# A hybrid encoder layer: the mixer walked head by head, or block by block

## The chip, the cores and the metric

One core of a Trainium2 chip runs the whole layer in one launch. The metric is device microseconds of one execution. Before the change three runs gave a median of 3042.16 us (3032.88 to 3047.0).

## What is computed

The input is 2048 tokens of width 1024. The layer normalises them (`layer_norm`), mixes them along the sequence, attends to 256 memory tokens and applies a squared-ReLU MLP, each with a scaled residual and a LayerNorm:

```python
h   = layer_norm(x, ln_in_g, ln_in_b)
mix = hybrid_mixer(h, ...)                       # 4 mLSTM heads || 4 GLA heads, one in-projection
h   = layer_norm(ALPHA * h + mix, ln1_g, ln1_b)
xa  = memory_cross_attention(h, mem, wq, wk, wv, wo)
h   = layer_norm(ALPHA * h + xa, ln2_g, ln2_b)
ff  = squared_relu_mlp(h, w_ff1, w_ff2)
h   = layer_norm(ALPHA * h + ff, ln3_g, ln3_b)
```

In the mixer, `proj = h @ w_in` gives q, k, v and an output gate for each mLSTM head, q, k, v and a gate for each GLA head, and a few gate columns. Each head then runs a recurrence along the sequence in chunks: a state is carried from chunk to chunk, so within a head the order of time is fixed, while heads are independent of one another.

## The kernel before

**Number format.** A float32 value goes to TensorE (PE) as a pair of float16 tensors, high and low part; `mm3` (lines 149 to 154) multiplies a pair with a pair in three matmuls. Weights are brought into this form by `prep` (line 136): a load of 1 MB into the one staging tile `stg` (`load_stage`, line 117), the largest magnitude on VectorE (line 110) and over partitions on POOL (line 114), a power of two from it, the high part on ScalarE (line 129) and the low part on VectorE (line 130).

**The units.** The tokens stand in four blocks of 512. A unit is one mLSTM head, or a pair of GLA heads, on one block: 6 head groups, 24 units, listed in `units` (line 809) head group by head group, and within a group block by block. The step of unit u is the recurrence `rec(u)` followed by the in-projection of unit u+3 (`LOOK`, line 830). `m_inproj` makes q, k (with a short convolution), v and the gate of an mLSTM head; `g_inproj` does it for a GLA pair. `m_pre` (line 401) loads the broadcast rows mb and scb and forms the scores, `m_rec` (line 427) walks the chunks; `g_rec` (line 565) builds its decayed scores in seven levels. `y_out` stores the result (line 477). A head group's weights are prepared once, one to two units ahead, and stay in SBUF for its four blocks.

**The front.** All 16 token tiles are normalised first (`ln_in`, line 225), the transposed float16 pairs of the four blocks are kept in SBUF (`hT`), and `gates` and `gate_math` (line 332) compute the gate columns of all 2048 tokens. Beside this the kernel folds the cross-attention weights with the memory tokens: eight folds, each two preparations (`x_w`), `x_a` (keys or values of a head) and `x_b` (their product with the query or output weight), stored to DRAM. Four folds stand between the LayerNorm tiles, with two extra staging slabs for the first, and four in the first four steps of the loop:

```python
        for b in (2, 3):
            x_w(nx)
            x_a(nx)
            for i in range(CPB):
                ln_in(b * CPB + i)
            x_b(nx)
            nx += 1
            gates(b)
            inproj(b - 1)
        gate_math()
```

**The passage to the next stage.** After the last GLA unit of the list, eight units before the end, `b_out_weights` (line 745) and `b_x_weights` (line 774) prepare the output weights and load the folded weights; then `s1`, `s2`, `s3` run the output projection, the cross-attention and LayerNorms tile by tile, and the MLP follows.

**What sets the order.** The kernel is written as one program; when it is built, a scheduler orders each engine's instructions and the DMA queue of SP by program order as priority, as soon as operands and a free buffer are there in its own model of time. So an instruction may go ahead of earlier ones, within the number of buffers of its tile. On the chip each engine and queue runs its own order, waiting where something is late. Nearly all loads, stores and transposing DMAs go through SP's queue.

Of the kernel before, what the change touches and what calls it, by code (L numbers as in the profile page):

```python
# [9 lines left out]
F32 = mybir.dt.float32  # L10
# [26 lines left out]
PF0 = 2  # L37
PF = 1
MA = 0
XO = 1  # L40
GA = 2
XE = 1
NX = 5
NHS = 3
# [13 lines left out]
def layer_kernel(ctx: ExitStack, tc, a, out):  # L58
# [6 lines left out]
    wsp = ctx.enter_context(tc.tile_pool(name="wsp", bufs=4))  # L65
    big = ctx.enter_context(tc.tile_pool(name="big", bufs=4))
# [11 lines left out]

    def slab(shape, dt):
        return big.tile(shape, dt, name="slab")  # L80
# [10 lines left out]
    nm_d = dram.tile([64, P], F32, name="nm_d")  # L91
    sc_d = dram.tile([64, P], F32, name="sc_d")
    glr_d = dram.tile([16, T], F32, name="glr_d")
# [38 lines left out]
    def w_pair(pool=None):  # L132
        pool = pool or wsp
        return pool.tile([P, 2048], F16, name="whi"), pool.tile([P, 2048], F16, name="wlo")
# [76 lines left out]
    with ExitStack() as actx:  # L211
        ca = actx.enter_context(tc.tile_pool(name="ca", bufs=1))
        wk = actx.enter_context(tc.tile_pool(name="wk", bufs=2))
        WPOOL = False
        hT = [slab([P, CPB, 2, KC, P], F16) for b in range(2)]

        pxctx, p1ctx = ExitStack(), ExitStack()
        px = pxctx.enter_context(tc.tile_pool(name="px", bufs=1, reuse_waits="tile", side="right"))
        p1 = p1ctx.enter_context(tc.tile_pool(name="p1", bufs=1, reuse_waits="tile", side="right"))
        est = slab([P, 2, 2048], F32)  # L220
        ew = slab([P, 4, 2048], F16)
        gt, bt = gb_load(p1, a["ln_in_g"], a["ln_in_b"], "in")
        inv_h0, ai_h0 = ln_scale(gt, bt, "h0")

        def ln_in(i):
            x = p1.tile([P, D], F32, name="x", bufs=NX)
            nc.sync.dma_start(x, a["x"][i * P:(i + 1) * P, :])
            layer_norm(x, gt, bt)
            b, ii = divmod(i, CPB)
            hs = p1.tile([P, 2, D], F16, name="hs", bufs=NHS)  # L230
# [15 lines left out]
        li = p1.tile([64, P], F32, name="li")  # L246
        lf = p1.tile([64, P], F32, name="lf")
        gbias = p1.tile([64, 2], F32, name="gbias")
# [14 lines left out]
        def gates(b):  # L263
# [3 lines left out]
            gs = p1.tile([48, TB], F32, name="gs")  # L267
            nc.scalar.activation(gs, pg[0:48, :], AF.Copy, scale=inv_g[0:48])
            for h in range(4):
                for r, dst in ((h, li), (4 + h, lf)):  # L270
                    nc.sync.dma_start(dst[h * 16 + b * 4:h * 16 + b * 4 + 4, :],
                                      gs[r:r + 1, :].rearrange("o (c t) -> o c t", c=4))
            nc.sync.dma_start(glr_d[:, b * TB:(b + 1) * TB], gs[32:48, :])
# [21 lines left out]
        def m_weights(h):  # L295
            qk = prep(a["w_mix"][2 * h], inv_h0, WPOOL)
            vo = prep(a["w_mix"][2 * h + 1], inv_h0, WPOOL)
            return qk, vo

        def m_inproj(h, b, w):  # L300
            (qh, ql, qv), (vh, vl, vv) = w
            qk = []
            for j in range(2):
# [4 lines left out]
                else:  # L308
                    nc.gpsimd.tensor_copy(raw[:, 0:3], raw_prev[j])
                raw_prev[j] = wk.tile([P, 3], F32, name=f"halo{j}")  # L310
                nc.gpsimd.tensor_copy(raw_prev[j], raw[:, TB:TB + 3])
# [18 lines left out]
        gcols = {}  # L330

        def gate_math():
            x = p1.tile([64, P], F32, name="gm_x")
            y = p1.tile([64, P], F32, name="gm_y")
            bb = p1.tile([64, P], F32, name="gm_b")
            one = p1.tile([64, P], F32, name="gm_1")
            cc = p1.tile([64, P], F32, name="gm_c")
            nc.vector.memset(one, 1.0)
# [6 lines left out]
            nc.vector.tensor_tensor_scan(bb, one, x, 0.0, ALU.mult, ALU.add)  # L345
# [4 lines left out]
            nc.tensor.transpose(pr[0:1, 0:64], bb[:, P - 1:P], ident[0:64, 0:64])  # L350
            nc.tensor.transpose(pr[0:1, 64:128], cm[:, P - 1:P], ident[0:64, 0:64])
            row = p1.tile([1, 5 * 64], F32, name="gm_row")
            nc.vector.tensor_copy(row[:, 0:128], pr[0:1, 0:128])
            nc.vector.tensor_tensor(row[:, 128:192], row[:, 0:64], row[:, 64:128], ALU.add)
            for h in range(4):
                nc.vector.tensor_tensor_scan(row[:, 192 + h * 16:192 + h * 16 + 16], row[:, h * 16:h * 16 + 16],
                                             row[:, 128 + h * 16:128 + h * 16 + 16], 0.0, ALU.add, ALU.max)
            nc.vector.memset(row[:, 256:320], 0.0)
            nc.vector.tensor_copy(row[:, 256:320].rearrange("p (h c) -> p h c", h=4)[:, :, 1:16],
                                  row[:, 192:256].rearrange("p (h c) -> p h c", h=4)[:, :, 0:15])  # L360
            pc = ps_s()
            nc.tensor.matmul(pc[0:64, 0:1], lhsT=row[:, 256:320], rhs=one[0:1, 0:1], start=True, stop=True)
# [762 lines left out]
```

## Time and profile before

| | |
|---|---|
| median of three runs | 3042.16 us (3032.88 to 3047.0) |
| profiled execution | span 3025.0 us from first to last instruction; its own time is not given beside it |
| PE busy | 2802.6 us |
| VectorE (DVE) busy | 1898.4 us |
| ScalarE (ACT) busy | 886.2 us |
| POOL busy | 416.1 us |
| mean granted TensorE clock | 0.963 |

A row of a window gives, for each engine, the us in which it was busy and the number of its instructions, then the granted clock of PE (1.00 is 2.4 GHz, 0.50 is 1.2 GHz), the mean busy share of the 16 DMA engines, and GB/s. A timeline row gives start and duration in us, engine, line and operation; what stands in brackets is the idle time before it and who ended it. Busy times of PE cover pipelined matmuls and are not a measure of its peak.

### The profile page before, as it was taken

What the parts mean: (1) busy time and instruction counts of PE and PEld (TensorE: products, weight loads), DVE (VectorE), ACT (ScalarE), POOL (GpSimd) and SP (SyncE); (2) the same over time, 40 slices, a digit from 0 to 9 for tenths busy, and PEclk for the clock granted to TensorE, in tenths of its full rate; (3) what the DMA queues carried; (4) which work ended last, traced back from release to release, by engine and by line L of the source; (5) the groups of instructions that cost most, each with busy time, mean ns of one, the idle gap of its engine ahead of it and who ended that gap; (6) DMA issues with size and microseconds to landing.
All of it is one profiled execution on the core that took longest, in us unless ns stands there. A gap on an engine that the chain in (4) does not pass through costs nothing.

```text
span 3025.0 us, 40992 instructions
## 1 busy us (share of the span) xinstructions
PE 2802.6 (93%) x16666; PEld 1576.8 (52%) x16666; DVE 1898.4 (63%) x3875; ACT 886.2 (29%) x1281; POOL 416.1 (14%) x565
## 2 busy tenths in 40 slices
PE   3579989989988898999999999999999999999997
PEld 2346667665666674565565444444444444444442
DVE  8946774656777666665665555555555555555468
ACT  3335444434445443223232211111111111111110
POOL 1102123323433221111111000000000000000011
PEclk8789999989999999999999999999999999999998
DMA  7832230100012334333437600000000000000001
GB/s 241 241 112 86 105 104 29 38 25 23 9 42 68 125 122 105 82 107 91 112 103 190 181 28 28 28 28 28 17 26 15 28 29 28 28 28 28 15 32 80
DMA packets 221693, 214.63 MB, mean 71 GB/s; under 512 B 171760, under 2 KB 188672, under 8 KB 212800
## 3 DMA queue, kind: packets, MB, share of 16 engines
q1 hardware_dynamic: 214592, 186.84, 21.0%
q0 software_dynamic: 6912, 25.17, 2.3%
q8 instruction: 130, 2.13, 0.3%
q14 instruction: 59, 0.48, 0.0%
HBM read 119.44 MB, written 50.53 MB: 56 GB/s over the span
## 4 chain that ended last, share of the span: by engine, by line
PE 69%; DVE 15%; issue 6%; POOL 3%; DMA 3%; ACT 2%; SPq 1%; POOLq 0%; ACTq 0%; DVEq 0%
PE mm L152 12%; PE mm L154 12%; PE mm L153 12%; PE s L152 9%; PE s L154 9%; PE s L153 8%; PE o L152 1%; PE o L153 1%; PE o L154 1%; DVE wmx L110 1%; DVE st L181 1%; DVE qk L316 1%; SPq L204 1%; DVE wlo L130 1%; DVE slab L1036 1%
## 5 line engine op out<-in xcount | busy, mean ns | idle before, releaser
L1036 DVE SCALAR_TENSOR_TENSOR slab<-s,uiv,slab 128x512 f32<-128x512 f32 x512 | 371.4, 744 | 45.0 <-PE s L154 44.8
L152 PE MATMUL s<-whi,uh 128*128 128x512 f16 x1024 | 389.6, 380 | 5.8 <-ACT uh L129 5.1
L152 PE MATMUL mm<-h2T,whi 128*128 128x512 f16 x1024 | 389.3, 380 | 2.5 <-DMA h2T<-h_d 2.5
L154 PE MATMUL s<-whi,ul 128*128 128x512 f16 x1024 | 387.8, 380 | 1.7 <-DVE ul L130 1.7
L153 PE MATMUL s<-wlo,uh 128*128 128x512 f16 x1024 | 389.3, 380 | 0.0
L153 PE MATMUL mm<-h2T,whi 128*128 128x512 f16 x1024 | 389.2, 380 | 0.0
L154 PE MATMUL mm<-h2T,wlo 128*128 128x512 f16 x1024 | 389.1, 380 | 0.0
L981 DVE CUSTOM_DVE_ANT_0 z<-z 128x512 f32<-128x512 f32 x128 | 88.2, 689 | 427.0 <-ACT z L980 427.0
L980 ACT ACTIVATE z<-mm,winv 128x512 f32<-128x512 f32 x128 | 87.9, 687 | 883.7 <-PE mm L154 883.7
L154 PEld LDWEIGHTS <-wlo 128*128 128x128 f16 x2064 | 203.8, 99 | 182.0 <-issue 9.6
L153 PEld LDWEIGHTS <-whi 128*128 128x128 f16 x1808 | 179.1, 99 | 219.4 <-issue 33.1
L152 PEld LDWEIGHTS <-whi 128*128 128x128 f16 x1808 | 179.0, 99 | 216.1 <-issue 14.0
L152 PE MATMUL mm<-whi,slab 128*128 128x256 f16 x1024 | 279.9, 274 | 12.5 <-ACT whi L129 7.3
L153 PE MATMUL mm<-wlo,slab 128*128 128x256 f16 x1024 | 279.9, 273 | 2.7 <-DVE wlo L130 2.7
L154 PE MATMUL mm<-whi,slab 128*128 128x256 f16 x1024 | 279.9, 273 | 0.0
L110 DVE TENSOR_REDUCE wmx<-stg 128x1 f32<-128x2048 f32 (+1 forms) x63 | 141.8, 2252 | 59.6 <-DMA stg<-in_w_ff 31.2
L152 PEld LDWEIGHTS <-uh 128*128 128x128 f16 x1024 | 100.3, 98 | 127.7 <-ACT uh L129 7.3
L154 PEld LDWEIGHTS <-ul 128*128 128x128 f16 x1024 | 99.9, 98 | 124.9 <-DVE ul L130 5.2
L130 DVE SCALAR_TENSOR_TENSOR wlo<-stg,w_s,whi 128x2048 f16<-128x2048 f32 x58 | 136.5, 2354 | 45.2 <-ACT whi L129 45.2
L114 POOL PARTITION_ALL_REDUCE amx<-umx x64 | 23.0, 360 | 1024.9 <-DVE umx L987 1013.1
L153 PEld LDWEIGHTS <-uh 128*128 128x128 f16 x1024 | 100.3, 98 | 121.1 <-issue 1.1
L152 PE MATMUL mm<-slab,whi 128*128 128x512 f16 x384 | 151.2, 394 | 0.4 <-ACT sg L325 0.4
(333 smaller groups left out, 5277.7 us busy)
## 6 DMA issues: line engine op xcount, KB each, us to landing
stg<-in_w_ff SPq DMA_DIRECT2D x32, 1024.0 KB
stg<-in_w_x SPq DMA_DIRECT2D x14, 1024.0 KB
stg<-in_w_mix SPq DMA_DIRECT2D x14, 1024.0 KB
x<-in_x SPq DMA_DIRECT2D x16, 512.0 KB
h_d<-x SPq DMA_DIRECT2D x16, 512.0 KB
y_d<-yh SPq DMA_DIRECT2D x32, 256.0 KB
r<-h_d POOLq DMA_DIRECT2D x16, 512.0 KB, 3.8
h_d<-hs POOLq DMA_DIRECT2D x16, 512.0 KB, 3.0
```

The costliest lines, as they stand in the source:

```text
L110: nc.vector.tensor_reduce(dst, src, axis=AX.X, op=ALU.max, apply_absolute_value=True)
L114: nc.gpsimd.partition_all_reduce(r, mx, P, bass_isa.ReduceOp.absmax)
L130: nc.vector.scalar_tensor_tensor(lo, stg, s, hi, ALU.mult, ALU.subtract)
L152: nc.tensor.matmul(psum, lhsT=lh, rhs=rh, start=(i == 0), stop=False)
L153: nc.tensor.matmul(psum, lhsT=lh, rhs=rl, start=False, stop=False)
L154: nc.tensor.matmul(psum, lhsT=ll, rhs=rh, start=False, stop=(i == n - 1))
L181: nc.vector.bn_stats(st[:, i, :], x[:, i * 512:(i + 1) * 512])
L204: nc.sync.dma_start_transpose(dst, src)
L316: nc.vector.scalar_tensor_tensor(cv, raw[:, t:t + TB], cj[:, t:t + 1], cv, ALU.mult, ALU.add)
L980: nc.scalar.activation(z[:, f], pz, AF.Relu, scale=w1[2])
L981: nc.vector.tensor_tensor_reduce(z[:, f], z[:, f], z[:, f], 1.0, 0.0, ALU.mult, ALU.max, mx[:, f:f + 1])
L1036: nc.vector.scalar_tensor_tensor(acc[ii][:, ns], po, iv, acc[ii][:, ns], ALU.mult, ALU.add)
```

## The change

The list of units is turned round: all head groups of a block, then the next block, with mLSTM and GLA units alternating.

```diff
+LOOK = 3
+UNITS = (("m", 0), ("g", 0), ("m", 1), ("m", 2), ("g", 1), ("m", 3))
+LAST = (("g", 0), ("m", 0), ("g", 1), ("m", 1), ("m", 2), ("m", 3))
-        units = [u + (b,) for u in (("m", 0), ("m", 1), ("g", 0), ("g", 1), ("m", 2), ("m", 3)) for b in range(NB)]
+        units = [u + (b,) for b in range(NB) for u in (UNITS if b < NB - 1 else LAST)]
```

The 14 in-projection weights are prepared in block 0 and stored; in the other blocks each unit loads them again, one unit ahead, into five pairs of buffers (before, four):

```diff
+        def mix_w(n, b):
+            if b == 0:
+                hi, lo, v = prep(a["w_mix"][n])
...
+                nc.sync.dma_start(wmix_d[n][0], hi)
+                nc.sync.dma_start(wmix_d[n][1], lo)
+            else:
+                hi, lo = w_pair()
+                nc.sync.dma_start(hi, wmix_d[n][0])
+                nc.sync.dma_start(lo, wmix_d[n][1])
+            return hi, lo, wscale[n]
```

The front normalises four tiles; the other blocks' LayerNorms, gates and gate mathematics (now on 16 rows of one block, with the running maximum carried) stand in the loop. The folds start in the step in which block 3's gates are done, and the output weights are prepared in steps 7 to 11, stored, and loaded again after the loop:

```diff
+        for i in range(2):
             ln_in(i)
+        wcur[0] = unit_w(0)
...
+        gates(0)
+        inproj(0)
+        g_setup(p2)
+        gate_math(0)
+        for u in range(1, LOOK):
+            inproj(u)
...
+        for u in range(-3, len(units)):
+            if u >= 0:
+                if u + GA < len(units) and units[u + GA][0] == "g":
+                    g_gate(u + GA)
+                rec(u)
+            b, k = divmod(u + 3, NU)
+            if b + 1 < NB:
+                if k < 2:
+                    for i in range(2):
+                        ln_in((b + 1) * CPB + 2 * k + i)
+                if k == 2:
+                    gates(b + 1)
+                    gate_math(b + 1)
+                    if b + 1 == NB - 1:
+                        p1ctx.close()
+                        x_mem(pxctx.enter_context(tc.tile_pool(name="px", bufs=1, reuse_waits="tile")))
+                        x_w(0)
+            if u >= 0 and u + LOOK < len(units):
+                inproj(u + LOOK)
+            if 7 <= u < 12:
+                out_w(u - 7)
+            if ("w", nx) in xm:
+                x_a(nx)
+                x_b(nx)
+                nx += 1
+                if nx < 8:
+                    x_w(nx)
+        pxctx.close()
...
+    wo, inv_m, g1, b1, inv_h1, ai_h1 = b_out_weights(bw)
+    wqk, vo = b_x_weights()
+    s1(0, bw)
+    s1(1, bw)
```

Two blocks of `hT` are kept instead of four. The two early staging slabs and the folds' own staging tile go, so all preparations use the one tile `stg`. Several buffers are fewer (`NX` 5 to 3, `NHS` 3 to 1, `lx` 4 to 3, `lxh` and `lxl` 3 to 2, `v2` and `sg2` 3 to 2, the GLA score tiles 2 to 1), and the recurrent states of all heads are held at once. The pools of the later stages change sides in SBUF.

## Rows read from the trace of the kernel before

**Rows 1.** The page's busy times and shares of the span, all engines.

```profile
PE 2802.6 (93%) x16666; PEld 1576.8 (52%) x16666; DVE 1898.4 (63%) x3875; ACT 886.2 (29%) x1281; POOL 416.1 (14%) x565
```

**Rows 2.** Windows of the front and of the stages after the mixer.

```profile
core 0: us, PE busy (x) PEld busy (x) DVE busy (x) ACT busy (x) POOL busy (x), PEclk, DMA share, GB/s
0.00:150.00 150.00, 73.53 (x408) 44.52 (x408) 135.55 (x218) 51.15 (x52) 22.29 (x42) 0.83 0.80 241
1180.00:3025.00 1845.00, 1810.51 (x9059) 886.17 (x9056) 1079.83 (x2065) 376.60 (x551) 118.00 (x183) 0.99 0.20 57
```

**Rows 3.** Line 415, first matmuls of each mLSTM recurrence: count, durations, first and last start.

```profile
L415 PE MATMUL s<-qk,qk x128: 272/276/422, 248.0 to 1129.2; 128*128 128x128 f32 x128
```

**Rows 4.** Windows of the mixer's stretches, columns as in rows 2.

```profile
248.00:541.60 293.60, 265.61 (x1883) 193.16 (x1882) 193.30 (x451) 132.17 (x197) 73.63 (x95) 0.97 0.24 83
541.60:979.60 438.00, 398.27 (x3693) 281.86 (x3691) 301.84 (x727) 197.71 (x302) 149.22 (x167) 0.92 0.10 31
979.60:1108.70 129.10, 116.90 (x779) 83.47 (x777) 86.78 (x193) 64.44 (x95) 31.11 (x46) 0.95 0.36 124
```

**Rows 5.** Timeline of SP: y stores that end the 8th, 16th, 21st and 24th step.

```profile
541.55 0.39 SPq L477 DMA_DIRECT2D y_d<-yh  x1
...
979.58 0.39 SPq L477 DMA_DIRECT2D y_d<-yh  x1
...
1108.68 0.39 SPq L477 DMA_DIRECT2D y_d<-yh  x1
...
1161.90 0.53 SPq L477 DMA_DIRECT2D y_d<-yh  x1
```

**Rows 6.** Timeline of PE inside an in-projection: start, duration, operation.

```profile
1109.03 0.38 PE L153 MATMUL mm<-slab,whi 128*128 128x512 f16 x1
1109.24 0.38 PE L154 MATMUL mm<-slab,wlo 128*128 128x512 f16 x1
1109.46 0.27 PE L152 MATMUL mm<-whi,slab 128*128 128x256 f16 x1
1109.57 0.27 PE L153 MATMUL mm<-wlo,slab 128*128 128x256 f16 x1
```

**Rows 7.** Groups by line, 0 to 1300 us, DVE: LayerNorm of the input and weight preparation.

```profile
L110 DVE TENSOR_REDUCE wmx<-stg 128x1 f32<-128x2048 f32 x31 | 70.5, 2278 | 28.4 <-DMA stg<-in_w_mix 23.4 <-DMA stg<-in_w_x 4.9
...
L130 DVE SCALAR_TENSOR_TENSOR wlo<-stg,w_s,whi 128x2048 f16<-128x2048 f32 x26 | 61.3, 2363 | 21.6 <-ACT whi L129 21.6
...
L181 DVE BATCH_NORM_STATS2 st<-x 128x6 f32<-128x512 f32 x32 | 21.1, 673 | 0.3 <-DMA x<-in_x 0.3
...
L193 DVE SCALAR_TENSOR_TENSOR x<-x,rs,b_in 128x1024 f32<-128x1024 f32 x16 | 21.0, 1344 | 5.1 <-POOL rs L184 5.1
...
L192 DVE SCALAR_TENSOR_TENSOR x<-x,mv,g_in 128x1024 f32<-128x1024 f32 x16 | 20.4, 1276 | 0.0
...
L201 DVE TENSOR_TENSOR hs<-x,hs 128x1024 f16<-128x1024 f32 x16 | 19.4, 1217 | 0.3 <-ACT hs L200 0.3
```

**Rows 8.** Timeline of SP: two loads into the staging tile, back to back.

```profile
599.13 0.33 SPq L120 DMA_DIRECT2D stg<-in_w_mix  x1
...
614.33 0.35 SPq L120 DMA_DIRECT2D stg<-in_w_mix  x1
```

**Rows 9.** Timelines of SP and POOL, window of 3 us: a 2 MB burst ahead of scb.

```profile
1070.15 1.93 SPq L782 DMA_DIRECT2D slab<-wqk_d  x4
...
1074.89 0.32 SPq L408 DMA_DIRECT2D scb<-sc_d  x1
...
1079.30 1.38 POOL L412 TENSOR_TENSOR scb<-scb,qk 128x512 f32<-128x512 f32 x1 [0.64 <-DMA scb<-sc_d]
...
1073.00:1076.00 3.00, 3.00 (x22) 2.14 (x21) 1.70 (x8) 2.57 (x5) 0.87 (x1) 1.00 1.03 410
```

**Rows 10.** Waits of SP's queue, 160 to 1140 us: total, times, longest.

```profile
SPq L120 <- DVE wlo L130: 197.7, 18, 38.8
```

More of the change, by code (lines that the diff above doesn't have):

```diff
@@ L77, in ps_o @@
         return ps.tile([P, 512], F32, name="o", bufs=2)
+    big = [None]
+    wsp = [None]
     def slab(shape, dt):
-        return big.tile(shape, dt, name="slab")
+        return big[0].tile(shape, dt, name="slab")
     ident = const.tile([P, P], F32, name="ident")
@@ L330, in layer_kernel, with gate_math @@
         gcols = {}
[L332 to L338, printed above, removed]
+        mlast = [None]
+        def gate_math(b):
+            li, lf = gif.pop(b)
+            x = p1.tile([16, P], F32, name="gm_x")
+            y = p1.tile([16, P], F32, name="gm_y")
+            bb = p1.tile([16, P], F32, name="gm_b")
+            cc = p1.tile([16, P], F32, name="gm_c")
+            one = ones
             nc.vector.tensor_scalar(li, li, gbias[:, 0:1], None, ALU.add)
@@ L495, in g_setup @@
             nc.vector.tensor_copy(idm, ident)
-            G["one"] = p2.tile([P, P], F32, name="one")
-            nc.vector.memset(G["one"], 1.0)
-            G["AT"] = [[p2.tile([P, CPB, P], F32, name=f"AT{i}{j}") for j in range(2)] for i in range(2)]
+            G["one"] = ones
+            G["AT"] = [[p2.tile([P, CPB, P], F32, name=f"AT{j}") for j in range(2)]]
             for r_ in G["AT"]:
@@ L718, in x_b @@
             h, side = divmod(n, 2)
-            w1, w2, wo_ = xm.pop(("w", n))
+            w1, w2 = xm.pop(("w", n))
             kh, kl = xm.pop(("k", n))
             oh, ol = (t.rearrange("p (k n) -> p k n", k=2) for t in w2[:2])
-            if wo_:
-                hi, lo = (wo_.tile([P, 2048], F16, name=f"xo{j}", bufs=1) for j in range(2))
-            else:
-                hi, lo = w_pair()
+            hi, lo = x_pair()
             for u in range(4):
@@ L743, in x_b, with out_w @@
             nc.sync.dma_start(dst[1], lo)
+        wo_d = [dram.tile([2, P, 2048], F16, name=f"wo_d{i}") for i in range(4)]
+        wsc_o = {}
+        def out_w(step):
+            if step < 2:
+                stg = load_stage(a["w_out"][step])
+                wsc_o["mx", step] = mx = sm.tile([P, 1], F32, name=f"womx{step}")
+                absmax(mx, stg)
+                if step == 0:
+                    return
+                mx1 = sm.tile([P, 1], F32, name="wmx")
+                nc.vector.tensor_tensor(mx1, wsc_o["mx", 0], mx, ALU.max)
+                wsc_o["m"] = pow2(all_max(mx1), "wo", bufs=1, pool=const)
+                i, s = 1, wsc_o["m"][0]
+            elif step == 2:
+                stg = load_stage(a["w_out"][0])
+                i, s = 0, wsc_o["m"][0]
+            else:
+                i = step - 1
+                stg = load_stage(a["w_out"][i])
+                mx1 = sm.tile([P, 1], F32, name="wmx")
+                absmax(mx1, stg)
+                s, v = wsc_o[i] = pow2(all_max(mx1), f"wo{i}", bufs=1, pool=const)
+            hi, lo = w_pair()
+            split_with(stg, s, hi, lo)
+            nc.sync.dma_start(wo_d[i][0], hi)
+            nc.sync.dma_start(wo_d[i][1], lo)
@@ L745, in b_out_weights @@
         def b_out_weights(bw):
             wo = [None] * 8
[L747 to L756 removed]
+            for i in range(4):
@@ L828, in rec @@
                 g_rec(h, b, blks.pop(u), u)
-        LOOK = 3
-        x_mem()
-        x_w(0, True, False)
+        ones = ca.tile([P, P], F32, name="ones")
+        nc.vector.memset(ones, 1.0)
         for i in range(2):
             ln_in(i)
-        x_a(0)
+        wcur[0] = unit_w(0)
         for i in range(2, CPB):
             ln_in(i)
-        x_b(0)
-        x_w(1, True)
         gates(0)
-        for i in range(CPB, CPB + 2):
-            ln_in(i)
-        x_a(1)
-        for i in range(CPB + 2, 2 * CPB):
-            ln_in(i)
@@ new lines, in layer_kernel @@
+        g_setup(p2)
+        gate_math(0)
+        for u in range(1, LOOK):
+            inproj(u)
+        for u in range(min(GA, len(units))):
+            if units[u][0] == "g":
+                g_gate(u)
+        nx = 0
+        NU = len(UNITS)
+        for u in range(-3, len(units)):
[20 more added lines that the diff above has]
+            if ("w", nx) in xm:
```

312 lines of the change are left out of this document (128 added, 184 removed).

## Prediction

> **What bounds the kernel now.** I read the page's busy shares first, then the windows by stage, then the stretches of the mixer, and last the rows that price its steps. TensorE (PE) is busy for most of the span [rows 1], so the question is where it is not. From 1180 us on it is busy 1810.5 of 1845 us at clock 0.99 [rows 2]; the change touches nothing there but pool places, so I cost that stage at nothing. The slack lies before. In the first 150 us PE is busy 73.5 us at a granted clock of 0.83, while VectorE (DVE) is busy 135.6 us, 90% [rows 2]: this stretch is DVE's, for all 16 input LayerNorms stand in it and the first recurrence starts only at 248.0 us [rows 3]. After that PE is busy some 90%: 265.6 of 293.6 us, 398.3 of 438 us at clock 0.92 (the GLA recurrences), 116.9 of 129.1 us [rows 4]. So there are two places to gain: work that could run while the LayerNorms run, and the GLA stretch.
>
> **Prices of the steps before.** A step is the recurrence of unit u with the in-projection of unit u+3. The stores of y mark them [rows 5]. Five steps with mLSTM (m) in both parts take 979.58 to 1108.68 us: 25.8 us each. The last three, without in-projection, take 53.2 us. Matmuls of 512 columns follow each other every 0.215 us, those of 256 every 0.11 us [rows 6], so a GLA (g) in-projection (48 and 192 matmuls) is 10.5 us longer than an m one (48 and 96). The eight g recurrences take 438.0 us, 54.75 each; five of them run beside a g in-projection, so a g recurrence costs 54.75 - 25.8 - 5/8 x 10.5 = 22.4 us more than an m one. The first eight steps take 541.55 - 248.0 = 293.5 us; 8 x 25.8 + 3 x 10.5 = 237.9 of them are plain steps, which leaves 55.6 for the four weight folds of that stretch with their weight preparation: 13.9 us a fold. (PE's own part of a fold is 96 matmuls of 256 columns, 10.5 us, so this price is some PE work and a little wait.)
>
> **Part one, the front.** Only four tiles are normalised before the first in-projection, and block 1's four beside units 1 to 3. A LayerNorm tile costs DVE 2 x 0.673 + 1.276 + 1.344 + 1.217 and small ones, 5.6 us; preparing a weight costs it 2.28 + 2.36 and five small operations, 5.3 us [rows 7]. All 14 mixer weights are now prepared in block 0. DVE's work until unit 5's step begins: units 0 to 4 at the DVE time per step of the m and g stretches, 86.8/5 = 17.4 and 301.8/8 = 37.7 us [rows 4], 3 x 17.4 + 2 x 37.7 = 128; 14 x 5.3 = 74; eight tiles, 45; convolutions of units ahead and set-up, some 16: together 263 us. At the 90% that DVE reached before in such a stretch this ends at 291 us. The other bound, the one staging tile, is nearer than it was, since the second staging slab goes: two loads into it stand 15.2 us apart [rows 8], 14 x 15.2 = 213 us, and the mask and gate weights some 15 more. It ends earlier, so DVE sets 291 us.
>
> **Part two, the rest of the mixer.** From unit 5 there are 16 steps with an in-projection, 5 of them of g, 6 g recurrences, and the three last: 16 x 25.8 + 5 x 10.5 + 6 x 22.4 + 53.2 = 653 us. The pairs g with g and m with m become g with m and m with g, which in these prices gives the same sum. All eight folds come here (before, four stood in the LayerNorm front, where PE was idle): 8 x 13.9 = 111 us. The gate projections of blocks 2 and 3: 2 x 24 x 0.215 = 10 us. The gate mathematics, four short chains on 16 partitions for one on 64, and the LayerNorms of blocks 2 and 3 (45 us of DVE) I cost at nothing: they are issued three units or more ahead, beside stretches where DVE is busy 66 to 69% [rows 4]; uncovered they would be 45 us. Sum: 291 + 653 + 111 + 10 = 1065 us for the last y store, against 1161.9 before [rows 5]: 97 us less.
>
> **Part three, what is added.** First, 14 MB of stored weights and 42 MB of reloads (two 0.5 MB halves per weight, 18 units). DMA was busy 10 to 36% in these stretches [rows 4]; 56 MB over 1065 us is 53 GB/s, and a burst of 2 MB ran at 410 GB/s [rows 9]. The bytes are hidden. What could show is the queue: SP issues in its order, and a reload that waits for a free weight pair holds up the mb and scb loads of the next recurrence, on which POOL, then DVE, then PE wait. Before, a load waiting for the staging tile held SP 197.7 us in 18 times, 11 us each [rows 10], while scb was used 4.4 us after its issue, after a wait of 0.6 us behind a 2 MB burst [rows 9]. Bounds: 0 (the pair was freed a unit earlier) and 18 x 8 = 144 us (11 less some 3 us of slack). I take 12, nearer to 0, because five pairs hold any two neighbouring units and the burst row shows 0.6. Second, the folds: the two halves now follow each other at once, and 12 steps (8 m, 4 g, 290 us of DVE) get 8 x 2 x 5.3 = 85 us of it for fold weights, 5 x 4.6 = 23 for the output weights and 22 of LayerNorm: 420 of some 550 us, 76%, and the folds' evictions on top. Bounds 0 and 60 (one idle chain of 7 us per fold); I take 20, as in the steps with folds before DVE was busy 66% and PE still 90% [rows 4]. Third, the passage to the next stage: output weights, fold results and LN1 vectors, some 13 MB, are loaded only when the mixer's pools are free. At 410 GB/s that is 32 us; their places come free with the last in-projection, about the 53 us of the last three steps earlier. Bounds 0 and 32; I take 12.
>
> Gain 97 - 12 - 20 - 12 = 53, rounded down to 52 us. The profile's span is 3025.0 us; the execution's own time is not given beside it, the median of the three runs lies 17.2 us above it (the fastest 7.9), and I keep 17.2 as what lies around the span and between runs: 3025 - 52 + 17 = **2990 us**.
>
> **The rivals.** (a) *The mixing fills the gaps of the GLA stretch.* For it: PE is idle 40 of 438 us and its clock 0.92 there [rows 4], and now every g recurrence has m units around it. Against: only three buffers of q, k and v let units run ahead, and PE's order is fixed at build. If a g recurrence cost only some 12 us over an m one, six of them save 60: 2930 us. The Trainium skill's page Perfetto Trace Analysis, section Optimization Strategy, advises interleaving regimes that have different busiest engines, which is this rival. By that rule the trace agrees for the front (90% DVE), while in the GLA stretch DVE at 69% was no full regime of its own.
> (b) *The cover is lost.* Passage and folds both cost their upper bounds, 32 and 60 us, and block 0 slips by a few: nothing is left, about 3040 us. For it: one staging tile for everything, and a fold's chain crosses five engines. Against: steps with folds before, at 13.9 us a fold.
> (c) *Slower: the reloads block SP.* Place: SP's queue, ahead of the mb and scb loads. Price: 8 us in each of the 18 reloading units, 144 in place of my 12, so 80 us over before: about 3122 us; milder, 3080. It decides from 3.6 us a unit on, where the remaining gain of 64 us is gone. For it: the 11 us holds [rows 10]. Against: the 0.6 us [rows 9]. The Trainium skill's page DMA: Bandwidth & Descriptors, section Queues, rings and completion order, says that each DMA engine consumes a sequencer's descriptors in ring order, which speaks against the change: a 3 MB reload ahead of scb would then cost its full 7.5 us at the measured rate, 135 us in 18 units, so about 3113 us. By that rule the trace agrees only in part: scb behind 2 MB was 0.6 us late.
> (d) That it does not do what it says: the blocks are walked by the new unit list, so only the order of issue could keep the old front; I give it no chance of its own.
>
> **How the numbers follow.** Forecast 0.45, (a) 0.17, (b) 0.18, (c) 0.20. Around the forecast the bounds of part three reach about +/- 40 us. The range runs from (a) at 2930 to the milder half of (c), 3085; left out are half of (a) and half of (c), just under 0.2. About 0.5%, 15 us, is what a measurement can tell from no change here. Faster by more: 0.45 x 0.95 + 0.17 + a little of (b), 0.62. Slower by more: (c) and a little of (b), 0.23. Between: 0.15. The forecast's own range is 2950 to 3030.
>
> **What would show it.** Right: the first recurrence's matmuls near 100 us, the fifth y store before 300, the last near 1110; DVE near 90% until 290; the stage after it as long as before. Part two is wrong if steps between reloads are longer than 26 us (m). Rival (c) shows as POOL or DVE waiting for the mb or scb load, and SP's waits on weight reloads; (b) as PE waiting for kh or for the output weights. A last y store after 1162 makes the prediction wrong.

## Result: slower by 3.4%, and the profile after

The changed kernel takes 3140.56 us (median of four runs, 3134.47 to 3162.05) against 3044.58 us for the kernel before on the same chip: a ratio of 1.0338, 95% interval 1.0292 to 1.0384. The prediction was 2990 us; it was wrong in sign, and the time lies above its range of 2930 to 3085. The profiled span is 3134.0 us, 109 us more than before. Busy time of the engines, from the page, beside [rows 1]:

```profile
PE 2815.1 (90%) x16696; PEld 1585.3 (51%) x16696; DVE 1897.4 (61%) x3956; ACT 909.7 (29%) x1312; POOL 424.0 (14%) x563
```

TensorE is busy 12.5 us longer than before, VectorE as long as before. So some 96 of the 109 us are new idle time of TensorE. Windows of the changed kernel by stage, columns as in [rows 2] (time, length, then busy time of PE, PEld, DVE, ACT and POOL, granted clock, DMA share, GB/s):

```profile
0.00:54.60 54.60, 0.00 (x0) 0.11 (x1) 36.55 (x67) 12.06 (x10) 7.08 (x17) 1.00 0.71 213
54.60:393.00 338.40, 263.58 (x1883) 174.52 (x1883) 231.24 (x507) 140.02 (x195) 80.76 (x101) 0.84 0.49 156
393.00:1190.60 797.60, 692.94 (x5496) 492.79 (x5495) 502.64 (x1194) 357.79 (x527) 201.06 (x247) 0.92 0.34 113
1190.60:1256.60 66.00, 21.61 (x117) 16.44 (x116) 26.63 (x90) 17.71 (x26) 11.47 (x13) 0.67 0.91 310
```

There are two holes. In the first 54.6 us TensorE does nothing. Between the last in-projection (1190.6 us) and the first output projection (1256.6 us) it works 21.6 of 66 us, while the DMA engines are at 0.91 of their time: they carry what the next stage needs. Who TensorE waited for up to the first output projection (total us, times, longest):

```profile
PE mm L152 <- DMA hT<-hs: 54.6, 1, 54.6
PE mm L152 <- DMA whi<-y_d: 36.6, 1, 36.6
PE mm L152 <- ACT whi L129: 30.2, 5, 11.1
PE o L471 <- DVE mb L451: 21.6, 9, 12.4
PE s L152 <- DVE AT L622: 16.1, 11, 6.2
PE mm L152 <- ACT kh L129: 12.8, 4, 8.2
...
PE o L473 <- POOL scb L446: 9.8, 3, 5.0
...
PE mm L152 <- DVE xw L760: 8.1, 5, 3.0
PE s L379 <- DVE gm_b L374: 6.7, 1, 6.7
```

The first line is the empty start: the first transposed LayerNorm tile. The second is the passage, the third a weight that is not yet prepared. Then come the mLSTM's decay matrix mb, the GLA matrix AT, the folds (kh, xw), the scaled queries scb and the gate mathematics. Of the marks that the prediction named, the first recurrence's matmuls start at 210.0 us (line 449 of the changed kernel), not near 100. The others are in SP's timeline: first and last load of a mixer weight into the staging tile, the store of unit 4's y (the fifth unit), and the passage.

```profile
23.09 0.78 SPq L120 DMA_DIRECT2D stg<-in_w_mix  x1
...
317.52 0.38 SPq L120 DMA_DIRECT2D stg<-in_w_mix  x1
...
392.93 2.94 SPq L511 DMA_DIRECT2D y_d<-yh  x2
...
1191.24 1.45 SPq L819 DMA_DIRECT2D slab<-wqk_d  x3
...
1223.37 0.39 SPq L511 DMA_DIRECT2D y_d<-yh  x1
...
1224.89 0.48 SPq L798 DMA_DIRECT2D wo_h<-wo_d  x1
...
1238.71 11.04 SPq L204 DMA_TRANSPOSE whi<-y_d  x1
```

The 14 loads take 294.4 us, 22.6 us from one to the next on average; between the fifth and the sixth the GLA mask also goes through the tile. The fold results (slab) are asked for as soon as the last in-projection has ended, the output weights (wo_h), which are needed first, only after the last y store, and the first transposed y tile after them. The vector updates of the output projection, after and before (durations, then first and last start):

```profile
L837 DVE SCALAR_TENSOR_TENSOR r<-mm,inv_m,r x32: 742/750/751, 1257.2 to 1715.9; 128x512 f32<-128x512 f32 x32
L837 DVE SCALAR_TENSOR_TENSOR r<-mm,inv_y,r x64: 741/750/752, 1258.5 to 1719.7; 128x512 f32<-128x512 f32 x64
```

```profile
L800 DVE SCALAR_TENSOR_TENSOR r<-mm,inv_m,r x32: 717/748/751, 1135.8 to 1608.3; 128x512 f32<-128x512 f32 x32
L800 DVE SCALAR_TENSOR_TENSOR r<-mm,inv_y,r x64: 720/751/754, 1138.1 to 1612.1; 128x512 f32<-128x512 f32 x64
```

Before, the output projection began 26 us ahead of the last y store (1161.9 us, [rows 5]); now it begins 34 us behind it. So the error of the prediction, 161 us on the span (3134.0 against 2973), divides like this:

| stretch | predicted | measured | error |
|---|---|---|---|
| start to the fifth unit's y store | 291 | 392.9 | +102 |
| from there to the last y store | 774 + 20 + 12 = 806 | 1223.4 - 392.9 = 830.5 | +24 |
| last y store to the last update of the output projection | 450.2 as before, + 12 | 1719.7 - 1223.4 = 496.3 | +34 |
| the rest | 1412.9 as before | 1414.3 | +1 |

### The profile page after: what moved, and what is told of

It reads as the page before. It is cut to its first block, busy times and chain, and to the rows that moved or that the text cites. A ratio compares the mean times of both kernels' runs of the same rounds, so it can differ in the third digit from the quotient of the medians.

```text
span 3134.0 us, 41376 instructions
## 1 busy us (share of the span) xinstructions
PE 2815.1 (90%) x16696; PEld 1585.3 (51%) x16696; DVE 1897.4 (61%) x3956; ACT 909.7 (29%) x1312; POOL 424.0 (14%) x563
## 4 chain that ended last, share of the span: by engine, by line
PE 68%; DVE 14%; DMA 6%; issue 5%; ACT 4%; POOL 3%; SPq 0%; POOLq 0%; ACTq 0%; DVEq 0%
PE mm L152 12%; PE mm L154 12%; PE mm L153 12%; PE s L154 8%; PE s L153 8%; PE s L152 8%; PE o L152 2%; PE o L153 2%; PE o L154 2%; DMA stg<-in_w_mix 2%; DVE wmx L110 1%; DVE wlo L130 1%; DVE qk L344 1%; DVE st L181 1%; DVE xw L130 1%
## 5 line engine op out<-in xcount | busy, mean ns | idle before, releaser
L152 PE MATMUL s<-whi,uh 128*128 128x512 f16 x1024 | 389.9, 381 | 6.5 <-ACT uh L129 5.3
L152 PE MATMUL mm<-whi,hT 128*128 128x256 f16 x1024 | 283.2, 277 | 15.5 <-ACT whi L129 13.9
L152 PEld LDWEIGHTS <-whi 128*128 128x128 f16 x1664 | 164.5, 99 | 258.5 <-DMA whi<-y_d 36.9
L153 PE MATMUL mm<-wlo,hT 128*128 128x256 f16 x1024 | 283.0, 277 | 4.0 <-DVE wlo L130 4.0
L154 PE MATMUL mm<-whi,hT 128*128 128x256 f16 x1024 | 282.7, 276 | 0.0
L154 PEld LDWEIGHTS <-wlo 128*128 128x128 f16 x1920 | 189.2, 99 | 177.7 <-issue 6.8
L153 PEld LDWEIGHTS <-whi 128*128 128x128 f16 x1664 | 164.6, 99 | 212.8 <-issue 26.8
L110 DVE TENSOR_REDUCE wmx<-stg 128x1 f32<-128x2048 f32 (+1 forms) x66 | 148.8, 2254 | 79.1 <-DMA stg<-in_w_ff 35.4
L152 PE MATMUL mm<-hT,whi 128*128 128x512 f16 x384 | 152.3, 397 | 24.2 <-ACT whi L129 16.2
L154 PE MATMUL mm<-hT,wlo 128*128 128x512 f16 x384 | 151.1, 394 | 1.3 <-DVE wlo L130 1.3
```

What stands on the lines that cost most here:

```text
L110: nc.vector.tensor_reduce(dst, src, axis=AX.X, op=ALU.max, apply_absolute_value=True)
L152: nc.tensor.matmul(psum, lhsT=lh, rhs=rh, start=(i == 0), stop=False)
L153: nc.tensor.matmul(psum, lhsT=lh, rhs=rl, start=False, stop=False)
L154: nc.tensor.matmul(psum, lhsT=ll, rhs=rh, start=False, stop=(i == n - 1))
```

## The experiments

Fourteen kernels, in five groups; each group has its own runs of the kernel before, so ratios are compared, not times. 0.001 of the ratio is about 3 us. The changed kernel stands at 1.0338; it was not run again in these groups, and its own interval is 14 us wide to either side, so a difference from it is known to some 15 to 20 us.

**Two staging tiles.** The loads into the one staging tile alternate with a second one; its place is taken from the weight pairs.

```diff
-wsp[0] = ...tile_pool(name="wmx", bufs=5)
+wsp[0] = ...tile_pool(name="wmx", bufs=4)
+ws[0] = ...tile_pool(name="ws2", bufs=1)
...
-    stg = wst.tile([P, 2048], F32, name="stg")
+    ws[1] += 1
+    pool = ws[0] if ws[0] and ws[1] % 2 else wst
+    stg = pool.tile([P, 2048], F32, name="stg")
```

> A second staging tile for the weights during the mixer, paid for with one weight pair (four in place of five); DVE's work is the same. Theory F (the chain of fourteen loads through one staging tile, some 20 us a load, sets the front): the fifth y store falls from 392.9 us to about 300, the loads of the mixer weights end near 200 in place of 317, and the time falls by 60 to 90 us, to 3050 to 3080 us. Rival D (VectorE's work sets the front, as the prediction had it): the fifth store stays within 20 us of 393 and the time within 20 us of 3140. Rival Q (reloads on SP's queue are the loss): with a pair less they are issued later, so the time rises by 20 us or more.

Measured 3099.69 us, ratio 1.0215 (1.0197 to 1.0233): 0.0123 less, about 37 us. SP's timeline (last load of a mixer weight, the fifth unit's store, the last store) and TensorE's waits:

```profile
221.73 0.73 SPq L124 DMA_DIRECT2D stg<-in_w_mix  x1
...
373.94 2.94 SPq L516 DMA_DIRECT2D y_d<-yh  x2
...
1179.11 0.39 SPq L516 DMA_DIRECT2D y_d<-yh  x1
```

```profile
PE mm L156 <- DMA hT<-hs: 56.0, 1, 56.0
PE mm L156 <- DMA whi<-y_d: 36.5, 1, 36.5
...
PE mm L156 <- ACT whi L133: 11.6, 1, 11.6
...
PE o L476 <- DVE mb L456: 3.8, 5, 1.4
...
PE o L478 <- POOL scb L451: 3.6, 2, 1.9
```

The wait for prepared weights (whi) falls from 30.2 to 11.6 us. The single staging tile did cost time, but theory F had its place only half right: the last load comes 96 us earlier (221.7 in place of 317.5), yet the fifth unit's store comes at 374, only 19 us earlier, and not at 300. So the chain of loads did not set the front by itself. By that store alone rival D, VectorE, would still stand; its bound of 20 us on the whole time does not hold. More than half of the gain in the profile comes later, up to the last y store (1223.4 to 1179.1 us), where TensorE's waits for mb and scb all but vanish (21.6 and 9.8 to 3.8 and 3.6 us). The empty start and the passage stand as they were.

**The control: four pairs.** Only the pairs, with one staging tile.

```diff
-wsp[0] = ...tile_pool(name="wmx", bufs=5)
+wsp[0] = ...tile_pool(name="wmx", bufs=4)
```

> The control to the run before: four weight pairs in place of five, still one staging tile. Theory F: the pairs are not what is waited for, 3140 us within 15, and the fifth y store at 393 within 10. Rival Q: each reload waits a part of a unit longer for its pair and holds up SP's queue, 2 to 4 us in each of 18 reloading units: 3175 to 3210 us.

3134.8 us, ratio 1.0328 (1.0303 to 1.0353): no difference to the changed kernel. No worth of the fifth pair shows while there is one staging tile, and rival Q's price for a missing pair, 35 us or more, falls.

**Output weights early.** The pools' sides are exchanged, and three of the four pairs of output weights are loaded after the last fold.

```diff
+                else:
+                    pxctx.close()
+                    wo_load(b2ctx.enter_context(tc.tile_pool(name="bwa", ..., side="right")), range(3))
-        pxctx.close()
```

> The mixer's pools change sides, so that three of the four pairs of output weights go to the places of the fold weights and are loaded after the last fold, and the fourth pair and the LN1 vectors go where the last in-projection's input stood. Theory P (the passage: the output weights are loaded last, behind 8 MB of fold results, and all TensorE work of the next stage waits for them): the first output projection starts before the last y store in place of 33 us after it, and the time falls by 40 to 60 us, to 3080 to 3100 us. Rival B (it is the bytes: 12 MB after the last in-projection take their time in any order): at most 10 us less, 3130 to 3140 us.

3140.41 us, ratio 1.0355 (1.0320 to 1.0391): no gain. TensorE's longest wait between 1180 and 1290 us, then SP's timeline, then the updates:

```profile
PE o L152 <- DMA wlo<-whi: 34.1, 1, 34.1
```

```profile
1226.42 0.99 SPq L822 DMA_DIRECT2D slab<-wqk_d  x2
...
1238.72 12.49 SPq L822 DMA_DIRECT2D slab<-vo_d  x8
1252.21 8.74 SPq L204 DMA_TRANSPOSE wlo<-whi  x1
```

```profile
L840 DVE SCALAR_TENSOR_TENSOR r<-mm,inv_m,r x32: 718/749/754, 1217.3 to 1717.6; 128x512 f32<-128x512 f32 x32
```

The first output projection did start 40 us earlier (1217.3 in place of 1257.2), and the wait for the first y tile is gone (0.6 us). But TensorE then waited 34.1 us for the next thing in SP's order, the transposed tile of the normalised result (wlo), which was asked for behind 8 MB of fold results. The last update is where it was. Theory P named the right place and too little of it.

**The passage put in order.** The GLA pool stands on the side that is closed first, so that all of the next stage's small things find a place there after the last GLA recurrence; the second half of the fold results (vo) is asked for after the first two tiles.

```diff
+            if u == 20:
+                pxctx.close()
+                p2ctx.close()
+                bw = b2ctx.enter_context(tc.tile_pool(name="bw", ..., side="right"))
+                wo, inv_m, g1, b1, inv_h1, ai_h1 = b_out_weights(bw)
...
-    wqk, vo = b_x_weights()
+    wqk = b_x_weights(ts, 0)
     s1(0, bw)
     s1(1, bw)
+    vo = b_x_weights(ts, 1)
```

> The run with early output weights only handed the wait on: TensorE next waited 34 us for a transposed tile that stood in SP's queue behind 8 MB of fold results. Here the GLA pool stands on the other side and is closed after the last GLA recurrence, so that all output weights, the LN1 vectors and the residual tiles go there, and the fold results for the second part are asked for after the first two tiles of the next stage. Theory P (it is the order in which SP asks, and the places): the first output projection starts before the last y store, TensorE's longest wait between 1180 and 1280 us falls below 20 us, and the time is 35 to 55 us less, 3085 to 3105 us. Rival B (12 MB after the last in-projection take their time in any order): again no gain, 3130 to 3145 us.

3119.23 us, ratio 1.0254 (1.0213 to 1.0295): 0.0084 less, about 26 us, short of the 35 to 55 that theory P wanted. TensorE's longest wait of the passage, and the updates:

```profile
PE o L152 <- DMA wlo<-whi: 10.1, 1, 10.1
```

```profile
L841 DVE SCALAR_TENSOR_TENSOR r<-mm,inv_m,r x32: 743/748/754, 1238.9 to 1711.8; 128x512 f32<-128x512 f32 x32
L841 DVE SCALAR_TENSOR_TENSOR r<-mm,inv_y,r x64: 721/751/754, 1240.8 to 1714.8; 128x512 f32<-128x512 f32 x64
```

From the last in-projection (here 1212.2 us) to the last update it is 502.6 us, where the changed kernel needs 1719.7 - 1190.4 = 529.3: the passage is 27 us shorter, with the same bytes, and rival B falls. The first output projection came at 1238.9, ahead of the last y store (1259.8). In this profile the last in-projection ended 22 us later, and the profiled run gained only 9 us; why is open. The 26 us are the difference of the ratios, so that they agree with the 27 is not proof that they are the same.

**Reloads twice, and reloads on another queue.**

```diff
     nc.sync.dma_start(hi, wmix_d[n][0])
     nc.sync.dma_start(lo, wmix_d[n][1])
+    nc.sync.dma_start(hi, wmix_d[n][0])
+    nc.sync.dma_start(lo, wmix_d[n][1])
```

> Every reload of a stored weight is made twice, so 42 MB more go through SP's queue. Theory F with P (reloads are hidden, in bytes and in the queue): 0 to 20 us more, 3140 to 3160 us, and the steps after the fifth y store as long as before. Rival Q (reloads hold up the small loads of the recurrences in SP's queue): the second copy costs 3 to 8 us in each of 18 reloading units, 3195 to 3285 us.

3164.81 us, ratio 1.0424 (1.0401 to 1.0446): 0.0086 more, some 26 us for 42 MB, 1.4 us in each of 18 units: more than theory F with P allowed, and about half of the least that rival Q wanted. If the first copy costs what the second does, reloads are worth about 26 us, an estimate. In these profiles the granted clock from 393 to 600 us was 0.91 here and 0.97 in the changed kernel, but also 0.93 in the kernel with the passage put in order, whose edit leaves the reloads alone and which slipped there by 14 us too (17 here); how much of the 26 is the copies' own is open. The second kernel of this pair loads once, by another queue:

```diff
-    nc.sync.dma_start(hi, wmix_d[n][0])
-    nc.sync.dma_start(lo, wmix_d[n][1])
+    nc.gpsimd.dma_start(hi, wmix_d[n][0])
+    nc.gpsimd.dma_start(lo, wmix_d[n][1])
```

> The reloads of the stored weights are issued by POOL in place of SP; bytes and buffers are the same. Theory Q2 (a part of the loss, some 20 us, is SP held by reloads ahead of the small mb and scb loads): TensorE's waits that go back to mb and scb fall from 31 to about 10 us and the time by 10 to 25 us, 3115 to 3130 us. Rival H (whoever issues them is held in its order; POOL then is late with the products of the recurrence): 10 to 60 us more, 3150 to 3200 us.

3178.67 us, ratio 1.0444 (1.0415 to 1.0472): 0.0106 more, about 32 us. One of TensorE's largest waits in this kernel, then POOL's longer wait for weight pairs:

```profile
PE s L152 <- DVE AT L622: 36.4, 15, 6.2
```

```profile
POOL wlo L321 <- PE mm L154: 58.1, 9, 16.1
```

The wait for the GLA matrix AT, whose inputs POOL helps to multiply, rises from 16.1 to 36.4 us. This is as rival H said: a load that waits for a weight pair holds up whoever issues it, and theory Q2 falls. TensorE's waits for mb and scb stay at 24.8 us (31.4 in the changed kernel), where Q2 wanted 10. POOL is also busy 52 us longer, with 84 instructions more (476.1 against 424.0 us); what the holding and what the issuing costs is not separated.

**Room for the first LayerNorms.** On top of the control:

```diff
-NX = 3
-NHS = 1
+NX = 4
+NHS = 2
```

> Four weight pairs in place of five (the control, 3135 us), and the place used for two halves-tiles and four input tiles of the input LayerNorm in place of one and three. Theory L (the change's cut of these buffers from three and five to one and three makes the first four LayerNorm tiles a chain of about 10 us each through the transposing DMA, and TensorE waits 54.6 us for it): the first matmul comes before 42 us, the fifth y store 10 to 20 us earlier, and the time is 10 to 25 us below the control, 3110 to 3125 us. Rival F (the staging tile's chain alone sets the front): the first matmul comes earlier, but the fifth store and the time stay within 8 us of the control.

3142.24 us, ratio 1.0329 (1.0299 to 1.0359), the control's own. TensorE's waits in the control and here:

```profile
PE mm L152 <- DMA hT<-hs: 54.8, 1, 54.8
...
PE mm L152 <- ACT whi L129: 29.2, 5, 12.3
```

```profile
PE mm L152 <- ACT whi L129: 42.4, 8, 12.2
PE mm L152 <- DMA hT<-hs: 40.9, 1, 40.9
```

The empty start shrank by 13.9 us, and the wait for weights grew by 13.2; the fifth unit's store stayed (390.5 and 389.3 us). As rival F said, the gain at the start is given back.

**Gate mathematics a unit later.** What follows it at this place, the folds' set-up, moves along.

```diff
     gates(b + 1)
+if k == 3:
     gate_math(b + 1)
```

> The gate mathematics of blocks 1 to 3 is issued one unit after the gate projection, in place of right behind it (the folds, which follow it, start a unit later too). Theory G (TensorE stands in its order behind the small transposes of the gate chain, 22 us of waits in the mixer): these waits fall below 10 us and the time by 8 to 20 us, 3120 to 3132 us. Rival N (the waits only change their names, as VectorE is late in the same places): 3140 us within 8.

3139.2 us, ratio 1.0314 (1.0289 to 1.0339): 0.0024 less, within both intervals. Undecided alone, nearer to rival N.

**The gains together.** Two staging tiles and the passage put in order, in one kernel, by the diffs above; then with the later gate mathematics; then that with a second halves-tile, paid for by a GLA buffer and a y buffer:

```diff
-NHS = 1
+NHS = 2
...
-x = p2.tile([P, TB], F32, name="lx", bufs=3)
+x = p2.tile([P, TB], F32, name="lx", bufs=2)
...
-yh = rk[0].tile([P, CPB, 2, P], F16, name="yh")
+yh = rk[0].tile([P, CPB, 2, P], F16, name="yh", bufs=1)
```

> The second staging tile (1.0215 of the time before when alone) and the passage with output weights loaded early (1.0254 alone) together; four weight pairs. If the two losses are separate (theories F and P), their gains of 1.2 and 0.8% against the changed kernel (1.034) add: a ratio of 1.010 to 1.016, about 3075 us. Rival W (the front's gain is spent waiting at the next stage anyway, since both end in the same queue): 1.018 to 1.024.

> The run before, with the gate mathematics one unit later. Alone that moved nothing, as the staging tile's chain set the front; with the second staging tile TensorE waits some 30 us for gate chains. Theory G: with staging out of the way these waits now count, ratio 0.004 to 0.008 below the run before. Rival N: within 0.003 of it.

> The run before, with two halves-tiles for the input LayerNorm in place of one (room from one buffer less of a GLA tile and of the y halves). Alone, with one staging tile, the wait for the first transposed tile fell from 54.6 to 40.9 us and TensorE gave it back waiting for weights. Theory L: with two staging tiles it is not given back, ratio 0.003 to 0.006 below the run before. Rival: the buffers taken away cost as much, within 0.002 of it or above.

The first gave 1.0123 (1.0095 to 1.0151), 3070.06 us: the two gains add, and rival W falls. The second gave 1.0087 (1.0063 to 1.0111), 3060.28 us: 0.0036 less, just between what rival N allowed and theory G wanted, and the intervals overlap; undecided. The third gave 1.0143 (1.0117 to 1.0170), worse by 0.0056: TensorE's wait for lxh, which is made from the tile that lost a buffer, rises from 32.6 to 49.3 us and its wait in the passage from 9.5 to 24.4, while the empty start shrinks only from 57.5 to 54.5.

A fourth, on top of the second, gives the first block's LayerNorms four input tiles and four halves-tiles in the place where the GLA pool is opened afterwards, so that nothing else shrinks.

```diff
+        p0 = p0ctx.enter_context(tc.tile_pool(name="p0", bufs=4))
...
         for i in range(2, CPB):
             ln_in(i)
+        p0ctx.close()
+        p2 = p2ctx.enter_context(tc.tile_pool(name="p2", bufs=1, reuse_waits="tile"))
```

> On top of the run with two staging tiles, early output weights and later gate mathematics (ratio 1.0087): the four tiles of block 0 get their own input tiles (four) and halves-tiles (four) in the place where the GLA pool is opened afterwards, so nothing else gets smaller. Theory L (the single halves-tile makes the first LayerNorms a chain, and TensorE waits 57 us for it): the first matmul comes before 45 us and the ratio falls to 1.000 to 1.005. Rival S (the first transposed tile is then waited for by DMA bandwidth or by VectorE, which also prepares weights there): the first matmul stays above 50 us, ratio 1.007 to 1.010.

3068.02 us, ratio 1.0111 (1.0086 to 1.0136): no gain. Window and waits of this kernel:

```profile
0.00:40.00 40.00, 0.00 (x0) 0.00 (x0) 33.71 (x65) 11.02 (x9) 5.09 (x15) 1.00 0.79 250
```

```profile
PE mm L156 <- DMA hT<-hs: 47.5, 1, 47.5
...
PE mm L156 <- ACT whi L133: 16.7, 3, 13.8
```

The start is 10 us shorter (57.5 in the kernel that it stands on), between what theory L and rival S wanted, and VectorE is now busy 33.7 of the first 40 us: LayerNorms and weights share it, and what one gains the other waits for (whi 16.7 us, which the kernel below it did not wait for). These buffers do not empty the start at a gain; whether other work could fill it was not tried.

**What was in that start before.** Before, it held weight folds. Two kernels leave the folds out: in `x_a` and `x_b` of either kernel only the scale and the stores of the fold weight are kept.

```diff
-            pk = ps_mm()
...
-            nc.vector.tensor_scalar(iv, w2[2], v, float(2 ** 23), ALU.mult, ALU.mult)
+            nc.vector.tensor_scalar(iv, w2[2], w1[2], float(2 ** 23), ALU.mult, ALU.mult)
...
-            hi, lo = x_pair()
-            for u in range(4):
...
+            hi, lo = w1[:2]
```

> The changed kernel without the weight folds: their weights are still loaded, prepared and stored, but the matmuls, evictions and scale chains of the eight folds are left out (the output is not the reference's). By PE's own part, 8 x 10.5 = 84 us, and its 28 us of waits in the fold chains, theory U (in the last block nothing hides them) expects 85 to 110 us less than 3140: 3030 to 3055 us, ratio 0.998 to 1.006. Rival V (they fill TensorE's gaps there): under 60 us, 3080 us or more.

> The kernel before without the weight folds, left out in the same way (the output is not the reference's). Theory U: the four folds of the LayerNorm front were hidden there, so only the other four are saved with part of the waits: 35 to 65 us less, ratio 0.979 to 0.988, and the stretch to the first recurrence shortens by less than 15 us. Rival V: they cost the same in either place, 85 to 110 us less, ratio 0.964 to 0.972.

Changed kernel: 1.0039 (1.0021 to 1.0058), so its folds cost 0.0299, about 91 us. Kernel before: 0.9832 (0.9801 to 0.9864), so there they cost 0.0168, about 51 us. Without folds the last y store of the changed kernel goes from 1223.4 to 1137.9, and the fifth unit's from 392.9 to 389.9:

```profile
389.87 2.94 SPq L511 DMA_DIRECT2D y_d<-yh  x2
...
1137.93 0.39 SPq L511 DMA_DIRECT2D y_d<-yh  x1
```

In the kernel before, first and last y store without folds, and the first 150 us; then the first y store with them:

```profile
276.69 0.40 SPq L477 DMA_DIRECT2D y_d<-yh  x1
...
1117.21 0.53 SPq L477 DMA_DIRECT2D y_d<-yh  x1
```

```profile
0.00:150.00 150.00, 36.10 (x193) 20.23 (x194) 119.25 (x185) 44.00 (x39) 22.90 (x38) 0.85 0.75 231
```

```profile
278.40 0.40 SPq L477 DMA_DIRECT2D y_d<-yh  x1
```

With folds TensorE was busy 73.5 us in this window [rows 2], without them 36.1. The first recurrence's matmuls start 27 us earlier (220.6 in place of 248.0), more than the 15 that theory U allowed, yet the first y store comes only 1.7 us earlier. All four folds of the front are done by then (their last matmul starts at 214.6 us), so they were nearly free there; the saving grows beside the other four, to 45.0 us at the end of the eighth step and 44.7 at the last y store. In the main theory U holds: moving the folds cost about 91 - 51 = 40 us by the ratios, known to some 18 us either way, and 85.5 - 44.7 = 41 by the last y store.

## Why the prediction was wrong

**The step that failed is the bound of the front** ("It ends earlier, so DVE sets 291 us"). VectorE and the staging tile were looked at, and TensorE itself was left out. In the changed kernel it could do nothing for 54.6 us and then had 263.6 us of work to do before the fifth unit's store, since in-projections run three units ahead. That alone makes 54.6 + 263.6 = 318 us; the granted clock was 0.84 there, so part of this work ran at the lower of the two levels. The remaining 75 us are waits. One of their causes is the staging tile, which the prediction dismissed with 15.2 us a load, the back-to-back spacing of [rows 8]; measured were 22.6. The quickest round still took 15.2; in the slowest, 41.5 us, the weight's largest magnitude is ready at 293.9 us and VectorE comes to it at 308.8, after the recurrences' operations that stand before it in its order. A second tile gave 19 us there and 37 in all; with it the empty start and TensorE's own work are 56.0 + 258.3 = 314 of the 374 us. One rival in the front was not tried: the stores of the prepared weights, which are new, hold SP's queue for 82 us in 12 waits of the first 330 us, until the high part is ready. And VectorE was not at 90%: 36.6 + 231.2 = 267.8 of 393 us, 68%. Its work was sized well (263), its share not.

**The empty start** was costed at nothing. The cut of the LayerNorm buffers from five and three to three and one stood in the diff and was not priced; as the runs show, giving buffers back gains nothing, for when the start shrinks by 14 us the weights take them back. The comparison that should have been made is with what TensorE did in that time before: folds, 37 us of work in the first 150 us, at no cost.

**The folds.** The prediction saw that "before, four stood in the LayerNorm front, where PE was idle", and priced all eight at 13.9, 111 us. Part three added 20 for their crowding, 131 together. Measured were 85.5 us at the last y store, a little over TensorE's own 8 x 10.5. So these terms were too high by 46, and rival (b)'s fear for the fold chains did not come true: TensorE waited 12.8 us for kh and 8.1 for xw, where the kernel before waited longer for kh alone (its waits up to its first output projection):

```profile
PE mm L152 <- ACT kh L129: 44.7, 5, 14.6
```

**The middle** came out only 24 us above the sum, and that is luck: two errors cancel. Without folds it takes 1137.9 - 389.9 = 748 us, where the sum without its fold terms is 675. So the steps with their reloads were 73 us longer than priced, and the folds 49 us cheaper there. Longer steps were the prediction's own sign that part two is wrong. Of the 73, a second staging tile takes some 25 (44 us at the last y store less 19 at the fifth unit's), and reloads may be 14 above the 12 allowed, if their doubling is a measure. The rest has no run of its own. The GLA tiles that lost buffers in the change (lx, lxh, lxl, v2, sg2) are an untried rival: no run gives them back. The gate mathematics was costed at nothing; TensorE waited for it some 22 us in the mixer (sum over five groups, of which the largest is shown), but moving it gave no gain outside the intervals.

**Rival (c)** was right that it would be slower, but its mechanism shows only in small. Its sign is there: SP waits 133 us in 24 turns to issue reloads, and TensorE's waits for mb and scb are 31.4 us where before they were 7.9. But with two staging tiles these fall to 7.8 while SP waits for reloads as long as ever (136 us in 26 turns). The larger of SP's two waits, in the changed kernel and with two staging tiles:

```profile
SPq L321 <- PE mm L154: 95.7, 15, 9.9
```

```profile
SPq L326 <- PE mm L158: 95.8, 15, 9.8
```

So most of the small loads' lateness that reached TensorE went with the staging tile. To the reloads the traces put some 7 or 8 us of it: with every reload made twice these waits are 39.5 us, with the reloads on POOL 24.8. All of these are single profiles. From the Trainium skill, DMA: Bandwidth & Descriptors, section Queues, rings and completion order (each DMA engine consumes descriptors in ring order), the prediction took 7.5 us of delay for a reload in each of 18 units, 135 us. The 26 us measured for the second copies do not agree with that reading. Nor was its sum right: only the six GLA units reload 3 MB, so 42 MB at the 410 GB/s of [rows 9] make about 102 us, an estimate, and as much again for the second copies.

**The passage** was priced at 12 with a bound of 32. Measured against the old stage it cost 46 us from the last y store on (496.3 against 450.2), more than its bound of 32, which rival (b) took. From the last in-projection on it is 529.3 us against 492.5 before (1612.1 - 1119.6), 37 more, of which 27 come back when the same bytes are asked for in the order in which they are needed. What the prediction missed is above all the order: 13 MB at 410 GB/s are 32 us, and the weights that are needed first were asked for last. Its other premise failed too: the last in-projection ended 33 us before the last y store, not 53; before the change it was 42.

**Rival (a)**, that mixing fills the GLA gaps, did not show. TensorE is idle 104.7 of 797.6 us from the fifth unit's store to the last in-projection (13%), where it was idle 40 of 438 us (9%) in the GLA stretch before [rows 4]. The Trainium skill, Perfetto Trace Analysis, section Optimization Strategy, says beside its advice to interleave that a gap which keeps coming back can mean too little SBUF for the next tile; this case agrees, with 37 us for one more staging tile.

Put together: 37 us for the staging tile, 26 for the passage and 40 for the folds' place make 103 us, as much as was lost (0.0338, about 103 us). That it comes out even is chance: each item is known to some 15 to 20 us, and only the first two were shown to add. If it is right, the gain that was hoped for, twelve LayerNorm tiles out of the front, was spent on what remains: longer steps, reloads, gate mathematics, the empty start. This balance is an inference; no run shows each item alone. No version that does the whole work beats the kernel before; the nearest stands at 1.0087.

## What to carry to other kernels

When work is moved out of a stretch where the busiest engine had gaps, ask first what stood in those gaps at no cost: here four weight folds under the LayerNorms delayed the first y store by 1.7 us in their old place, and moving them cost some 40 us. Price a front by every engine, TensorE's own work included, and add the time until its first operand is there. At a border between stages the order in which one queue is asked matters as much as the bytes: write down what the first tile needs, in order, and give it a place that comes free early; and follow the whole chain of the first tile, since mending one link only moves the wait to the next.

## What was not expected of the hardware

A transfer of 42 MB more, where the DMA engines were busy a third to a half of the time, went with 26 us more, although TensorE had the same instructions to run. Reloads issued by POOL were slower by 32 us than the same reloads issued by SP. And four folds that keep TensorE busy for 37 us delayed the first y store by 1.7 us in the kernel before, while eight that keep it busy for 84 us cost about 91 in the changed kernel.
